# Making the row of inverse norms behind the first feature products in a hybrid RG-LRU and attention layer

## The chip, the cores and the metric

The kernel runs on one core of one Trainium2 chip. The metric is the time of one execution on the device, in microseconds (us). Engines are named as in the profile: PE is TensorE's matrix product (PEld its weight load), DVE is VectorE, ACT is ScalarE, POOL is GpSimd, SP is SyncE, whose queue issues most of the DMAs.

## The reference

One layer (DEPTH 1) over 2048 tokens of 1024 features, float32:

```python
h = rms_norm(x, norm1[l])
p = h @ w_in[l]
lru_x, lru_g, q, k, v, g, z = jnp.split(p, SPLIT_IDX, axis=-1)
lru_x = causal_depthwise_conv(lru_x, conv_w[l], conv_b[l])
lru_o = rg_lru(lru_x, ...) * jax.nn.gelu(lru_g)
...
o = gla_chunk_causal(qh, kh, vh, lah)
o = rms_norm(o, gla_norm[l]).reshape(bsz, seq, GLA_V)
gla_o = o * jax.nn.silu(g)
x = x + jnp.concatenate([lru_o, gla_o], axis=-1) @ w_out[l]
h = rms_norm(x, norm2[l])
gate, up = jnp.split(h @ w_ffn_in[l], 2, axis=-1)
x = x + (jax.nn.silu(gate) * up) @ w_ffn_out[l]
return rms_norm(x, final_norm)
```

What matters here is the first line. `rms_norm` divides each token's row by the root of its mean square and multiplies it by a gain. The division can be put behind the product with `w_in`, since it is one number per token.

## The kernel before

**Blocks and products.** The tokens are taken in four blocks (b = 0 to 3) of 512. Each product is float32 made of three passes: both operands are split into a high part (a rounding copy on ScalarE, CAST in the profile) and a low part (a subtraction on VectorE); `mm3` (L248 to L251) multiplies high by high, high by low and low by high. `split` (L256 to L260) makes the pair, so every weight and activation split has the line L259.

**Two kinds of product.** `feat` (L457) takes one unit of weights and gives a feature-major tile, 128 features by 512 tokens, in one PSUM bank: 8 chunks of 3 matmuls, 24 in all. `tokmaj` (L466) gives four token-major tiles at once, one for each 128 tokens, in four banks; it takes four units of weights and multiplies, for each unit, 2 chunks by 4 tiles by 3 matmuls, again 24. PSUM has eight banks, all from one pool (`bank`, L212).

**Weights.** `Units` (L359) feeds the units in a fixed order (`block_units`, L378): for a block the 4 units of k and z, 4 features of the recurrent part, 4 units of v, 2 features of q, then for block 0 the 4 features of the gelu gate and the 4 units of g, and for later blocks the units of the previous block's output projection among them. Each time a unit is taken, the next is loaded on SP and the second after the one taken is split, so two split units lie ahead. Weights and activations lie in two arenas, handed out in grains of 128 words a partition by `Space.alloc`; a buffer that was given back can be written once its last reader is done.

**The norm.** `Norm1` (L300) prepares the norm of one block. `chunk` (L313) splits the transposed x times the gain, which is h without the division. `scales` (L322) loads the block's four x tiles (L325), squares and sums each on ScalarE (`sumsq`, L220), makes the inverse root in eleven small VectorE operations (`rsqrt_parts`, L230), which gives `rs`, one number per token on the partitions, and then spreads it: four copies to `wide` (L335), four products of `wide` with the identity (L336), which put the numbers along the free axis in one bank, and a copy to `rb` (L339). Token-major results are multiplied by `rs`, feature-major ones by `rb`.

**Where it stands.** For block 0 `scales` is called at the end of `tokmaj_first` (L498), behind the products for k and z and ahead of the first feature product. For blocks 1 to 3 it is called in the mixer of the block before (L653), behind the products for v, the gates (`lru_gates`, L521: they run between the units of v, the last after them) and the recurrence (`lru_scan`, L537), and ahead of that block's q features (L658). Behind q come the state products (L673), and then `lru_out` in block 0 (four gelu features, L701) or `prev.half(0)` in later blocks (a `tokmaj` for half of the previous block's output projection, L715). The x tiles and the scans share the arena. In the next block k and z come first (L574), then the first recurrent feature and its convolution (L579), the transposes of z (L583), the second feature, and the small products of z (L592).

**Order.** The program is unrolled. A scheduler works out each engine's order when the kernel is built: by the order of the program, with later work ahead where it takes it to be ready sooner. `tc.issue_after(ins)` asks that what is traced inside is issued behind `ins` on that engine. On the chip each engine takes its instructions in that order and waits at the head for what is missing.

Of the kernel before, what the change touches and what calls it, by code (L numbers as in the profile page):

```python
# [15 lines left out]
P = 128  # L16
D = 1024
SEQ = 2048
T = 512
NB = SEQ // T  # L20
TT = T // P
# [157 lines left out]
def hybrid_layer_kernel(  # L179
# [20 lines left out]
    nc = tc.nc  # L200
# [3 lines left out]
    A = Arena(Space(cp.tile([P, A_GRAINS * GRAIN], F32, name="arena"), A_GRAINS), A_BORDER)  # L204
# [7 lines left out]
    def bank():  # L212
        return pp.tile([P, T], F32, tag="mm", name="mm", bufs=8)

    def small(n, name):
        return cp.tile([P, n], F32, tag=f"s{n}", name=name, bufs=10 if n < 16 else 6)

    def sumsq(dst, src, n):
        b = A.alloc(n // 2)
        nc.scalar.activation(b.ap.bitcast(BF16), src, AF.Square, accum_out=dst)  # L220
        A.free(b)

    def run(gen, n=None):
        while n is None or n > 0:
            if next(gen, run) is run:
                return
            if n is not None:
                n -= 1

    def rsqrt_parts(dst, ss, scale, n):  # L230
        v = small(n, "rv")
        nc.vector.tensor_scalar(v, ss[0], scale, EPS, op0=ALU.mult, op1=ALU.add)
        for more in ss[1:]:
            nc.vector.scalar_tensor_tensor(v, more, scale, v, op0=ALU.mult, op1=ALU.add)
        y = small(n, "ry")
        nc.vector.tensor_scalar(y.bitcast(I32), v.bitcast(I32), -0.5, 1597463007.0, op0=ALU.mult, op1=ALU.add)
        t = small(n, "rt")
        for it in range(3):
            nc.vector.scalar_tensor_tensor(t, y, -0.5, y, op0=ALU.mult, op1=ALU.mult)
            nc.vector.tensor_mul(t, t, v)  # L240
            nc.vector.scalar_tensor_tensor(dst if it == 2 else y, t, 1.5, y, op0=ALU.add, op1=ALU.mult)
            if it != 1:
                yield

    def rsqrt(*args):
        run(rsqrt_parts(*args))

    def mm3(ps, sh, sl, mh, ml, first, last, again=False):  # L248
        nc.tensor.matmul(ps, lhsT=sh, rhs=mh, start=first, stop=False, skip_group_check=again)  # L249
        nc.tensor.matmul(ps, lhsT=sh, rhs=ml, start=False, stop=False, skip_group_check=again)  # L250
        nc.tensor.matmul(ps, lhsT=sl, rhs=mh, start=False, stop=last, skip_group_check=again)  # L251

    def pair(n, low=False):
        return Pair(R, n, low)
# [16 lines left out]
    def load(src, n, low=False, queue=nc.sync):  # L271
        b = A.alloc(n, low)
        queue.dma_start(b.f(n), src)
        return b
# [14 lines left out]
    ident = cp.tile([P, P], F32, name="ident")  # L289
    rs2 = cp.tile([P, SEQ // P], F32, name="rs2")  # L290

    def cc(i):
        return col[:, i : i + 1]
# [6 lines left out]
    class Norm1:  # L300
# [18 lines left out]
            self.h.append(b)  # L319
            self.fetch()  # L320

        def scales(self):  # L322

            ss = small(TT, "ss")
            xs = [load(x_v[self.b * TT + t], D) for t in range(TT)]  # L325
            for t in range(TT):
                sumsq(ss[:, t : t + 1], xs[t].f(D), D)
            A.free(*xs)
            self.rs = cp.tile([P, TT], F32, tag="rs1", name="rs1", bufs=2)
            rsqrt(self.rs, [ss], 1.0 / D, TT)  # L330
            wide = A.alloc(T)
            ps = bank()
            for t in range(TT):
                w = wide.f(TT, P)[:, t, :]
                nc.vector.tensor_copy(w, self.rs[:, t : t + 1].to_broadcast([P, P]))  # L335
                nc.tensor.matmul(ps[:, t * P : (t + 1) * P], lhsT=w, rhs=ident, start=True, stop=True)  # L336
            A.free(wide)
            self.rb = A.alloc(T)
            nc.scalar.copy(self.rb.f(), ps)  # L339

# [116 lines left out]
    def feat(h):  # L457
        wb = feed.get()
        ps = bank()
        for c in range(KC):  # L460
            wh, wl = wb[c // 4].r(4, P)
            mm3(ps, wh[:, c % 4, :], wl[:, c % 4, :], *h[c].r(T), c == 0, c == KC - 1)
        A.free(*wb)
        return ps

    def tokmaj(h, n, between=()):  # L466
        pss = [bank() for _ in range(TT)]
        between = list(between)
        for kp in range(4):
            wb = feed.get()  # L470
            for i in range(2):
                wh, wl = wb[i].r(n)
                c = 2 * kp + i
                mh, ml = h[c].r(T)
                for t in range(TT):
                    s = slice(t * P, (t + 1) * P)
                    mm3(pss[t][:, :n], mh[:, s], ml[:, s], wh, wl, c == 0, c == KC - 1)
            A.free(*wb)
            if between:
                between.pop(0)()  # L480
        return pss

    def tokmaj_first(norm, n):

        pss = [bank() for _ in range(TT)]
        for kp in range(4):
            for _ in range(2):
                norm.chunk()
            wb = feed.get()
            for i in range(2):  # L490
                wh, wl = wb[i].r(n)
                c = 2 * kp + i
                mh, ml = norm.h[c].r(T)
                for t in range(TT):
                    s = slice(t * P, (t + 1) * P)
                    mm3(pss[t][:, :n], mh[:, s], ml[:, s], wh, wl, c == 0, c == KC - 1)
            A.free(*wb)
        norm.scales()  # L498
        return pss

    def lru_conv(b, f, ps, rb):
        raw = A.alloc(T)
        nc.vector.tensor_mul(raw.f(), ps, rb)
        ps = raw.f()
        buf = A.alloc(T)
        xc = buf.f(T)
        nc.scalar.activation(xc, ps, AF.Identity, scale=cc(C_CW + 12 + f), bias=cc(C_CB + f))
        hl = cp.tile([P, 3], F32, tag="halo", name="halo", bufs=8)
        nc.vector.tensor_copy(hl, ps[:, T - 3 : T])
        for s in (1, 2, 3):  # L510
            w = cc(C_CW + (3 - s) * 4 + f)
            nc.vector.scalar_tensor_tensor(xc[:, s:], ps[:, : T - s], w, xc[:, s:], op0=ALU.mult, op1=ALU.add)
            if b > 0:
                nc.vector.scalar_tensor_tensor(
                    xc[:, :s], halo[f][:, 3 - s : 3], w, xc[:, :s], op0=ALU.mult, op1=ALU.add
                )
        halo[f] = hl
        A.free(raw)
        return buf
# [49 lines left out]
    def mixer(b, norm, prev, side):  # L569


        kzb = A.alloc(TT * 272)
        kz = kzb.f(TT, 272)
        pss = tokmaj_first(norm, 272) if b == 0 else tokmaj(norm.h, 272, [lambda: run(side, 1)] * 4)  # L574
        h = norm.h
        for t, ps in enumerate(pss):
            nc.scalar.activation(kz[:, t, :], ps[:, :272], AF.Copy, scale=norm.rs[:, t : t + 1])
        rb = norm.rb.f()
        xcs = [lru_conv(b, 0, feat(h), rb)]  # L579
        run(side, 2)  # L580
        zps = bank()
        for t in range(TT):
            nc.tensor.transpose(zps[:16, t * P : (t + 1) * P], kz[:, t, 256:272], ident)  # L583
        nc.vector.tensor_copy(zta[:16, :], zps[:16, :])
        xcs.append(lru_conv(b, 1, feat(h), rb))
        run(side, 2)
        zfs = []
        for t2 in range(2):
            zf = bank()
            for i in range(2):  # L590
                t = 2 * t2 + i
                nc.tensor.matmul(zf[:, i * 256 : (i + 1) * 256], lhsT=zta[:, t * P : (t + 1) * P], rhs=wal,  # L592
                                 start=True, stop=True)
# [17 lines left out]
        for t2 in range(2):  # L611
            la = las[t2].f()
            sf = bank()
            for i in range(2):
                t = 2 * t2 + i
                nc.tensor.matmul(sf[:, i * 256 : (i + 1) * 256], lhsT=sfx, rhs=la[:, i * 256 : (i + 1) * 256],
                                 start=True, stop=True)
                for a in range(2):
                    nc.tensor.matmul(dview[:, a, 2 * t : 2 * t + 2],
                                     lhsT=la[:, i * 256 + a * P : i * 256 + (a + 1) * P], rhs=ind,  # L620
                                     start=True, stop=True)
# [26 lines left out]
        after = None  # L648
        if b + 1 < NB:
            after = Norm1(b + 1)  # L650
            after.fetch()
            after.fetch()
            after.scales()  # L653


        qs = []
        for a in range(2):
            ps = feat(h)  # L658
# [5 lines left out]
        for t2 in range(2):  # L664
            ups = [bank(), bank()]
            for i in range(2):
                t = 2 * t2 + i
                for hd in range(4):
                    for half in range(2):
# [5 lines left out]
                            lhsT=eks[t2].f()[s, i * 256 + hd * 64 : i * 256 + hd * 64 + 64],  # L675
                            rhs=vs[t].f()[s, hd * P : (hd + 1) * P],
                            start=True, stop=True,
# [3 lines left out]
            for i in range(2):  # L681
                t = 2 * t2 + i
# [37 lines left out]
        for t2 in range(2):  # L720
            ops = [bank(), bank()]
            for i in range(2):
                t = 2 * t2 + i
                st = sts[t].f(2, 2, P)
                for half in range(2):
                    for hd in range(4):
# [5 lines left out]
                            lhsT=qs[hd // 2].f()[s, t * P + half * 64 : t * P + half * 64 + 64],  # L732
                            rhs=st[s, half, hd // 2, :],
                            start=True, stop=True,
# [36 lines left out]
        for hd in range(4):  # L771
            ps = bank()
# [560 lines left out]
    for b in range(NB):  # L1333
        side = blocks[0].normed(b - 2) if b > 1 else iter(())
        prev, nxt = mixer(b, nxt, prev, side)
# [126 lines left out]
```

## Time and profile before

| | |
|---|---|
| median of 3 runs | 2123.89 us (2120.2 to 2124.61) |
| the profiled execution | 2116.92 us |
| its span in the profile | 2115.1 us |
| PE busy | 1996.0 us (94%) |
| DVE busy | 1357.6 us (64%) |
| ACT busy | 894.7 us (42%) |
| mean granted clock of TensorE | 0.974 of full speed |

All times in the rows are from the profiled execution, in us from the start of its span. A row of the timeline gives start, duration, engine, line, operation, output and input by name, and in brackets how long the engine had been idle before it and what ended that. Matmuls are pipelined: the distance between two starts is the price of one, not its duration. A product of float32 operands that are not split (L336, L592, L673, L878) leaves two records for each instruction.

### The profile page before, as it was taken

To read this page: it belongs to the slowest core of one execution; us is meant where nothing else is said; L and a number is where in the kernel's file an instruction comes from. 1 tells how busy PE (TensorE), PEld (TensorE's weight loads), DVE (VectorE), ACT (ScalarE), POOL (GpSimd) and SP (SyncE) were. 2 spreads that over 40 slices of the span, in tenths; PEclk is the share of its full clock that TensorE was granted. 3 is DMA by queue.
4 is the path that set the end of the run, shared out by engine and by line. 5 is a ranking of instruction groups with operands and counts; after the bars stand their busy time and mean duration, and the time that the engine had idled before them with its cause. 6 is when DMAs were issued, how large, how long until landed. Compare 5 with 4: busy or idle time off the path is not lost.

```text
span 2115.1 us, 26513 instructions
## 1 busy us (share of the span) xinstructions
PE 1996.0 (94%) x9424; PEld 1644.8 (78%) x9424; DVE 1357.6 (64%) x2411; ACT 894.7 (42%) x1513; POOL 179.4 (8%) x216
## 2 busy tenths in 40 slices
PE   7689689959998999999999999999999999999997
PEld 6568578848887887888888888888888788888876
DVE  5556555655565577656777787777776466565676
ACT  5635634662465455443344464444443211121232
POOL 0000000000000000000011101111110222222110
PEclk9889899979999999999999999999999999999999
DMA  5142145423542464466565665765765946745632
GB/s 213 60 135 97 50 141 169 165 66 118 170 150 93 136 201 156 142 194 204 182 204 187 215 194 176 236 206 195 233 214 184 393 154 209 238 149 173 228 127 80
DMA packets 215783, 361.61 MB, mean 171 GB/s; under 512 B 19921, under 2 KB 95970, under 8 KB 215650
## 3 DMA queue, kind: packets, MB, share of 16 engines
q1 hardware_dynamic: 201506, 312.71, 45.9%
q0 software_dynamic: 14144, 47.20, 5.9%
q8 instruction: 74, 1.21, 0.2%
q14 instruction: 59, 0.48, 0.1%
HBM read 252.88 MB, written 106.95 MB: 170 GB/s over the span
## 4 chain that ended last, share of the span: by engine, by line
PE 88%; DVE 4%; ACT 3%; DMA 2%; issue 2%; POOL 0%; POOLq 0%; SPq 0%; DVEq 0%; ACTq 0%
PE mm L249 29%; PE mm L250 28%; PE mm L251 28%; DMA arena_r<-w2c 1%; DMA arena<-x2d 1%; PE mm L878 1%; DVE arena L542 1%; DVE arena L1219 1%; ACT arena L220 0%; DVE arena L540 0%; ACT arena L638 0%; DVE arena L541 0%; PE mm L336 0%; DMA arena<-in_xt_dram 0%; PE mm L730 0%
## 5 line engine op out<-in xcount | busy, mean ns | idle before, releaser
L250 PE MATMUL mm<-arena_r 128*128 128x512 f32 (+1 forms) x2712 | 1047.9, 387 | 4.5 <-DVE arena_r L259 4.5
L249 PE MATMUL mm<-arena_r 128*128 128x512 f32 (+1 forms) x2667 | 1037.4, 390 | 9.1 <-DVE arena L1219 8.6
L251 PE MATMUL mm<-arena_r 128*128 128x512 f32 (+1 forms) x2715 | 1043.8, 386 | 0.0
L249 PEld LDWEIGHTS mm<-arena_r 128*128 128x128 f32 x2667 | 502.8, 189 | 128.4 <-DVE arena L1219 14.9
L251 PEld LDWEIGHTS mm<-arena_r 128*128 128x128 f32 x2715 | 511.9, 189 | 103.5
L250 PEld LDWEIGHTS mm<-arena_r 128*128 128x128 f32 x2712 | 511.6, 189 | 103.5 <-DVE arena_r L259 5.8
L259 ACT CAST arena_r<-arena 128x512 fp32r<-128x512 f32 (+1 forms) x515 | 305.1, 608 | 554.6 <-PE mm L250 247.7
L259 DVE TENSOR_TENSOR arena_r<-arena,arena_r 128x512 fp32r<-128x512 f32 (+1 forms) x509 | 336.5, 675 | 273.4 <-ACT arena_r L259 226.7
L1219 DVE TENSOR_TENSOR arena<-arena,mm 128x512 f32<-128x512 f32 x272 | 186.6, 687 | 143.4 <-PE mm L251 143.3
L1185 ACT CAST arena_r<-arena_r 128x896 fp32r<-128x896 f32 (+1 forms) x88 | 80.0, 916 | 285.6 <-PE mm L250 164.0
L1090 POOL DMA_DIRECT2D w2c<-arena x125 | 67.9, 544 | 762.3 <-ACT arena L1081 714.9
L1186 POOL TENSOR_TENSOR arena_r<-arena_r 128x896 fp32r<-128x896 f32 x40 | 84.9, 2123 | 320.9 <-PE mm L251 114.6
L259 ACT CAST arena_r<-swing 128x512 fp32r<-128x512 f32 x86 | 53.2, 621 | 94.7 <-PE mm L250 31.0
L336 PE MATMUL mm<-ident,arena 128*128 128x128 f32 x32 | 8.2, 438 | 86.8 <-issue 64.0
L336 PEld LDWEIGHTS mm<-ident,arena 128*128 128x128 f32 x32 | 7.1, 328 | 88.2 <-issue 65.0
L220 ACT ACTIVATE arena<-arena 128x512 bf16<-128x512 f32 (+1 forms) x66 | 48.2, 730 | 63.7 <-DVE arena L1219 38.8
L259 DVE TENSOR_TENSOR arena_r<-swing,arena_r 128x512 fp32r<-128x512 f32 x86 | 59.1, 688 | 24.7 <-ACT arena_r L259 17.8
L979 ACT COPY arena<-mm 128x512 f32<-128x512 f32 x98 | 57.2, 583 | 18.7 <-PE mm L251 17.8
L695 POOL COPY stc<-arena 128x256 f32<-128x256 f32 x4 | 3.7, 917 | 679.1 <-DVE arena L688 493.7
L1186 DVE TENSOR_TENSOR arena_r<-arena_r 128x896 fp32r<-128x896 f32 (+1 forms) x48 | 49.3, 1026 | 11.3 <-ACT arena_r L1185 11.2
L1002 DVE TENSOR_TENSOR arena<-mm,arena 128x512 f32<-128x512 f32 x41 | 28.3, 691 | 43.1 <-PE mm L251 43.1
L994 DVE TENSOR_TENSOR arena<-mm,arena 128x512 f32<-128x512 f32 x41 | 28.3, 690 | 35.9 <-PE mm L251 35.9
(216 smaller groups left out, 1585.7 us busy)
## 6 DMA issues: line engine op xcount, KB each, us to landing
arena_r<-w2c SPq DMA_DIRECT2D x148, 256.0 KB, 5.3
arena<-in_wgu_dram SPq DMA_DIRECT2D x144, 256.0 KB, 4.1
arena_r<-ad SPq DMA_DIRECT2D x80, 448.0 KB, 3.6
w2c<-arena POOLq DMA_DIRECT2D x125, 256.0 KB, 3.6
ad<-arena SPq DMA_DIRECT2D x120, 256.0 KB, 3.1
arena<-in_wf_dram SPq DMA_DIRECT2D x40, 512.0 KB, 3.8
arena<-in_wo_dram SPq DMA_DIRECT2D x32, 512.0 KB, 4.2
arena<-in_w_dram SPq DMA_DIRECT2D x40, 256.0 KB, 3.9
```

What stands on the lines that cost most here:

```text
L220: nc.scalar.activation(b.ap.bitcast(BF16), src, AF.Square, accum_out=dst)
L249: nc.tensor.matmul(ps, lhsT=sh, rhs=mh, start=first, stop=False, skip_group_check=again)
L250: nc.tensor.matmul(ps, lhsT=sh, rhs=ml, start=False, stop=False, skip_group_check=again)
L251: nc.tensor.matmul(ps, lhsT=sl, rhs=mh, start=False, stop=last, skip_group_check=again)
L259: b.ins = [nc.scalar.copy(hi, src).ins, nc.vector.tensor_sub(lo, src, hi.bitcast(F32)).ins]
L979: nc.scalar.copy(b.f(), ps[:, :n])
L994: nc.vector.tensor_add(u1.f(), pb[:, :n], u1.f())
L1002: nc.vector.tensor_mul(u1.f(), pa[:, :n], u1.f())
L1090: nc.gpsimd.dma_start(w2c[k][:, m, i * T : (i + 1) * T], part.f())
L1185: nc.scalar.copy(hi, v)
L1186: (nc.gpsimd if i == 1 else nc.vector).tensor_tensor(lo, v, hi.bitcast(F32), op=ALU.subtract)
L1219: nc.vector.tensor_add(c, c, ps)
```

## The change

`scales` is cut in two. `norms` keeps the loads, squares, inverse root and the four copies to `wide`, at the two places where `scales` stood. `row` does the four products, gives `wide` back and copies to `rb`; it is called in the block that uses the row, behind its first feature product, in block 0 behind its first two, and is issued behind the last matmul of the last of these products.

```diff
--- before.py
+++ after.py
@@ -245,10 +245,13 @@
     def rsqrt(*args):
         run(rsqrt_parts(*args))
 
+    latest = []
+
     def mm3(ps, sh, sl, mh, ml, first, last, again=False):
         nc.tensor.matmul(ps, lhsT=sh, rhs=mh, start=first, stop=False, skip_group_check=again)
         nc.tensor.matmul(ps, lhsT=sh, rhs=ml, start=False, stop=False, skip_group_check=again)
-        nc.tensor.matmul(ps, lhsT=sl, rhs=mh, start=False, stop=last, skip_group_check=again)
+        mm = nc.tensor.matmul(ps, lhsT=sl, rhs=mh, start=False, stop=last, skip_group_check=again)
+        latest[:] = [mm.ins]
 
     def pair(n, low=False):
         return Pair(R, n, low)
@@ -319,7 +322,7 @@
             self.h.append(b)
             self.fetch()
 
-        def scales(self):
+        def norms(self):
 
             ss = small(TT, "ss")
             xs = [load(x_v[self.b * TT + t], D) for t in range(TT)]
@@ -328,13 +331,18 @@
             A.free(*xs)
             self.rs = cp.tile([P, TT], F32, tag="rs1", name="rs1", bufs=2)
             rsqrt(self.rs, [ss], 1.0 / D, TT)
-            wide = A.alloc(T)
+            self.wide = A.alloc(T)
+            for t in range(TT):
+                nc.vector.tensor_copy(self.wide.f(TT, P)[:, t, :], self.rs[:, t : t + 1].to_broadcast([P, P]))
+
+        def row(self):
+
             ps = bank()
-            for t in range(TT):
-                w = wide.f(TT, P)[:, t, :]
-                nc.vector.tensor_copy(w, self.rs[:, t : t + 1].to_broadcast([P, P]))
-                nc.tensor.matmul(ps[:, t * P : (t + 1) * P], lhsT=w, rhs=ident, start=True, stop=True)
-            A.free(wide)
+            with tc.issue_after(latest[0]):
+                for t in range(TT):
+                    nc.tensor.matmul(ps[:, t * P : (t + 1) * P], lhsT=self.wide.f(TT, P)[:, t, :], rhs=ident,
+                                     start=True, stop=True)
+            A.free(self.wide)
             self.rb = A.alloc(T)
             nc.scalar.copy(self.rb.f(), ps)
 
@@ -495,7 +503,7 @@
                     s = slice(t * P, (t + 1) * P)
                     mm3(pss[t][:, :n], mh[:, s], ml[:, s], wh, wl, c == 0, c == KC - 1)
             A.free(*wb)
-        norm.scales()
+        norm.norms()
         return pss
 
     def lru_conv(b, f, ps, rb):
@@ -575,14 +583,16 @@
         h = norm.h
         for t, ps in enumerate(pss):
             nc.scalar.activation(kz[:, t, :], ps[:, :272], AF.Copy, scale=norm.rs[:, t : t + 1])
+        fps = [feat(h) for _ in range(2 if b == 0 else 1)]
+        norm.row()
         rb = norm.rb.f()
-        xcs = [lru_conv(b, 0, feat(h), rb)]
+        xcs = [lru_conv(b, 0, fps[0], rb)]
         run(side, 2)
         zps = bank()
         for t in range(TT):
             nc.tensor.transpose(zps[:16, t * P : (t + 1) * P], kz[:, t, 256:272], ident)
         nc.vector.tensor_copy(zta[:16, :], zps[:16, :])
-        xcs.append(lru_conv(b, 1, feat(h), rb))
+        xcs.append(lru_conv(b, 1, fps[1] if b == 0 else feat(h), rb))
         run(side, 2)
         zfs = []
         for t2 in range(2):
@@ -650,7 +660,7 @@
             after = Norm1(b + 1)
             after.fetch()
             after.fetch()
-            after.scales()
+            after.norms()
 
 
         qs = []
```

## Rows read from the trace of the kernel before

**Rows 1.** Busy times of 0 to 820 us; TensorE's timeline at its five stops.

```profile
0.00:820.00 820.00, 720.02 (x3824) 602.93 (x3825) 475.26 (x982) 420.91 (x715) 5.56 (x12) 0.94 0.41 134
...
30.04 2.05 PE L336 MATMUL mm<-ident,arena 128*128 128x128 f32 x8 [9.51 <-issue]
...
116.31 2.05 PE L336 MATMUL mm<-ident,arena 128*128 128x128 f32 x8 [27.54 <-issue]
...
270.10 2.08 PE L336 MATMUL mm<-ident,arena 128*128 128x128 f32 x8 [22.76 <-DVE arena L335]
...
476.51 2.04 PE L336 MATMUL mm<-ident,arena 128*128 128x128 f32 x8 [27.00 <-issue]
...
675.94 0.79 PE L250 MATMUL mm<-arena_r 128*128 128x512 f32 x1 [4.22 <-DVE arena_r L259]
```

**Rows 2.** Timeline of VectorE in gap 1: the last scans, the four spread copies.

```profile
102.88 2.33 DVE L542 TENSOR_TENSOR_SCAN arena<-arena 128x512 f32<-128x512 f32 x2
...
115.98 0.63 DVE L335 COPY arena<-rs 128x128 f32<-128x128 f32 x4
```

**Rows 3.** TensorE's timeline and, with its clock, one stretch: prices of matmuls.

```profile
120.66 0.40 PE L249 MATMUL mm<-arena_r,swing 128*128 128x512 f32 x1
...
121.80 0.39 PE L251 MATMUL mm<-arena_r 128*128 128x512 f32 x1
...
676.00:680.40 4.40, 4.40 (x11) 0.50 0.92 328
...
680.37 0.39 PE L249 MATMUL mm<-arena_r 128*128 128x512 f32 x1
...
397.10 1.03 PE L878 MATMUL mm<-ident,arena 128*128 128x128 f32 x8
...
130.28 1.98 PE L673 MATMUL mm<-arena 64*64 64x128 f32 x64
```

**Rows 4.** Weight splits on VectorE up to 90 us, and gap 1's timeline.

```profile
L259 DVE TENSOR_TENSOR arena_r<-arena,arena_r 128x512 fp32r<-128x512 f32 x17 | 11.5, 690 | 12.6 <-PE mm L250 6.6 <-ACT arena_r L259 3.1 <-PE mm L251 2.8
...
L259 DVE TENSOR_TENSOR arena_r<-arena,swing 128x512 fp32r<-128x512 f32 x5 | 3.4, 688 | 5.5 <-ACT swing L259 4.5 <-issue 1.0
...
L259 DVE TENSOR_TENSOR swing<-arena,arena_r 128x512 fp32r<-128x512 f32 x4 | 2.8, 688 | 1.3 <-PE mm L250 1.3
...
L259 DVE TENSOR_TENSOR swing<-arena,swing 128x512 fp32r<-128x512 f32 x2 | 1.4, 688 | 0.1
...
107.09 0.38 SPq L273 DMA_DIRECT2D arena<-in_wf_dram  x1
...
114.01 0.69 DVE L259 TENSOR_TENSOR arena_r<-arena,arena_r 128x512 fp32r<-128x512 f32 x1
...
132.19 0.50 PE L249 MATMUL mm<-arena_r,swing 128*128 128x512 f32 x1
```

**Rows 5.** Timeline around gap 2, VectorE and TensorE.

```profile
264.26 0.69 DVE L259 TENSOR_TENSOR arena_r<-arena,arena_r 128x512 fp32r<-128x512 f32 x1
...
285.94 0.50 PE L249 MATMUL mm<-arena_r 128*128 128x512 f32 x1
```

**Rows 6.** Timeline around gap 3; the page's row of such loads.

```profile
466.43 0.69 DVE L259 TENSOR_TENSOR arena_r<-arena,arena_r 128x512 fp32r<-128x512 f32 x1
...
472.35 1.98 SPq L273 DMA_DIRECT2D arena<-in_wo_dram  x2
...
arena<-in_wo_dram SPq DMA_DIRECT2D x32, 512.0 KB, 4.2
...
493.15 0.50 PE L249 MATMUL mm<-arena_r,swing 128*128 128x512 f32 x1
```

**Rows 7.** Timeline of the opening, VectorE and TensorE.

```profile
20.20 1.96 DVE L259 TENSOR_TENSOR arena_r<-arena,arena_r 128x512 fp32r<-128x512 f32 x3
...
44.92 1.99 PE L592 MATMUL mm<-arena 17*128 17x256 f32 x8
```

**Rows 8.** Timeline of VectorE in the last block.

```profile
675.86 0.69 DVE L660 SCALAR_TENSOR_TENSOR arena<-mm,arena 128x512 f32<-128x512 f32 x1
```

## The prediction, made before the change was run

> **What bounds the kernel now.** I read the idle column of the costliest groups first, then TensorE's own timeline for the places of that idle time, then the timeline of all engines in one such place, and last the weight subtractions and loads around each. TensorE is busy 94% of the span. Before 820 us it is idle for 100 us (720 of 820 are busy), and 91 of these sit in five stops. Four of them end at L336, the product that spreads the inverse norms into a row: 9.51, 27.54, 22.76 and 27.00 us, 86.8 us together. The fifth, 4.22 us, ends at a matmul that waited for a weight subtraction [rows 1]. I call the first the opening and the next three gaps 1 to 3; the fifth is the same place in the last block, where no next norm is made.
>
> What holds TensorE in gap 1 can be read in order of time: the scans (L542) run until 105.2; then come the x tiles, which are loaded into buffers that the scans give back, their squares and the inverse root; and the last spread copy (L335) ends at 116.6 [rows 2]. Not one of these operations feeds the products that stand behind L336 in TensorE's order: those read the current block's h. TensorE takes its matmuls in order, so 27 us of a chain for the *next* block stand in front of work that could run.
>
> **What the change removes.** In gaps 1 to 3 the row leaves its place; the chain itself (loads, squares, root, copies) stays where it is, with the same DMAs on the same queue. TensorE goes from the last matmul of the value stage straight to two q products, then the state updates, then the next feature products (block 0) or the output half (blocks 1, 2). At full clock a matmul starts every 0.228 us (five between 120.66 and 121.80), so a feature product of 24 costs 5.45 us; the state updates cost 1.9 us [rows 3].
>
> Gap 1: TensorE would be free at 88.8, through both q products at 99.7 and the states at 101.6. Are the next weights there? By 90 us VectorE has made 28 subtractions of 128x512 (17+5+4+2); the gate matrices, four feature units, four value units, four gates and two q units take 2+8+8+4+4 = 26. Two are left over: the first unit behind the states is ready, and it lasts until 107.1. Its successor is loaded only at 107.09 and subtracted at 114.01 to 114.70 [rows 4]. So TensorE stops for some 7.6 us and begins that second product at 114.7. Before, the first began at 132.19, hence the second at 137.6: 22.9 us earlier. From this go 2.2 us because the clock has fallen again after an idle stretch, 1.0 us for the row, which comes later, and 2 us, an estimate, because VectorE has then to catch up with evictions, states and subtractions at 0.69 us each. The clock's price is from the fifth stop: behind it the granted clock was 0.50, the lower level of 1.2 GHz, and ten matmuls from 675.94 to 680.37 took 4.43 us, against 2.28 at 2.4 GHz [rows 1, 3]. The row's price at full clock is that of eight transposing records, 1.0 us [rows 3]. Gap 1 gives 17.7 us.
>
> Gap 2: TensorE is free at 247.3, done with q and states at 260.1, and wants the first output weights, whose first subtraction ends at 264.95. The output half began at 285.94 [rows 5]: 21.0 earlier, less 2.2 and 1.0: 17.8 us.
>
> Gap 3: free at 449.5, done at 462.3, first weights at 467.12. The first unit lasts, at the low clock at first, until 474.7. The second unit is the later of two loads issued from 472.35 for 1.98 us, so at about 474; such a load lands after 4.2 us, and a cast of 0.6 and a subtraction of 0.69 make 479.8. Before, that second unit began at 493.15+5.45 = 498.6 [rows 6]. 18.8 earlier, less 2.2 and 1.0: 15.6 us.
>
> The opening: two feature products now stand ahead of the row. Their weights and those of a third are ready at 22.2 (three subtractions from 20.20), the first ones earlier, and TensorE is free at 20.5. Two products last until 31.4; the row itself could start at 30.04, so its copies are there [rows 1, 7]. So the 9.5 us are covered whole. Row 1.0, transposes of z 0.6 (an estimate from four of the eight records of [rows 3]) and a copy of about 0.7 make 33.7, where L592 started at 44.92 [rows 7]: 11.2 us. The second product's unit is taken ahead of the row, so one value-weight load on the sync queue and two casts are issued earlier; nothing else stands between on those queues.
>
> **What it adds.** In blocks 1 to 3 the first product's bank is held until row and copy (1.0+0.6 us) have passed, and the ScalarE instructions behind that copy wait with it. On TensorE the second product, 5.45 us, covers this. If that cover went, 1.6 us in each of three blocks, 5 us, would be paid. The wide buffer now lives from norm to row, and the row's buffer begins there: four grains in either case, one after the other. I cost this at nothing; between minus 5 and plus 5 us, since another place in the arena can bring a load forward or delay it by about one load (4.2 us [rows 6]).
>
> Sum: 17.7+17.8+15.6+11.2 = 62.3 us. What is late next is VectorE and the weight loads: with the gaps closed the same 475 us of VectorE work before 820 us lie in some 60 us less [rows 1]. Bounds for new waits are 0 and 10; I take 2, nearer to zero, because all that lies between the five stops has 9 us of idle TensorE, some of them before its first matmul [rows 1]. That leaves 60 us. The profiled execution took 2116.92 us (a span of 2115.1 and 1.8 around it), so it would be 2057; the median of the runs shown lies 7.0 above the profiled time, so the forecast is **2064**.
>
> **A rule against it.** The last block passes the same place, with the same eight banks, and stops for 4.22 us only [rows 1]; there the first eviction of q (L660) stands right behind the scans, at 675.86 [rows 8]. The Trainium skill, "Perfetto Trace Analysis", Optimization Strategy, says that a stop which repeats on the engine that should be saturated can mean that there is no room in SBUF or PSUM for the next tile. By that rule the gaps would come back as waits for banks, as in the first rival, and the sum would be 48 us; by the last block's row it is not so.
>
> **The rivals.** *Banks.* The q evictions could stand behind the inverse root on VectorE. Then q and the states hold six of eight banks, and the output half, which needs four, stands until both q banks are free. In gap 2 that is 270.1 (L336's start), then about five VectorE operations of 0.69: 273.5; in gap 3 476.5 and the same: 480. With half of the first twelve matmuls done, TensorE is then where it was at 287.3 and 494.5: gains of 13.8 and 14.5, less 2.2 and 1.0 each. With 11.2 for the opening and 15.7 for gap 1 (2 more of catching up), and 2 for new waits, 48 us: 2076. For it: VectorE takes its work in order. Against: [rows 8].
>
> *All hidden.* Each gap shrinks to the 4.22 us of the last block: 77.3 - 12.7 = 64.6, the opening 11.2, and three rows at 1.0 us instead of the 2.05 of the low clock 3: 79 us, 2045. Against it: the load at 107.09 and the second unit of gap 3 come late whatever TensorE does.
>
> *No change of order.* The order on each engine is worked out when the kernel is built; the row could still be put ahead of the products, and the time would stay at 2124. Against: only one matmul product is made to wait, and its place behind a named matmul is asked for.
>
> *Slower.* Place: the arena and the sync queue. The wide buffer could cut the free stretch in which weights (eight grains each) are loaded ahead, so that a load starts only when TensorE leaves the unit before. Price per unit: load 4.2, cast 0.6, subtraction 0.69 = 5.5 us of idle TensorE. From eleven units on it eats the 60 us; with 14 units the time is 2064+77 = 2141. Against it: the units are made two ahead, and the row's buffer held as many grains over the same stretch.
>
> **How the numbers follow.** Forecast 0.60, with a range of its own from 2054 to 2074 (the catching up and the new waits at their bounds); banks 0.18; all hidden 0.12; no change 0.04; slower 0.04; the last 0.02 for a small gain under 40 us. The range runs from 2045 to 2084: it takes in all hidden, the forecast and the banks with room for their own spread, and leaves out about 0.12. A measurement of this kernel can tell 0.2%, some 4 us, from no change. Faster by more: 0.92; within: 0.04; slower: 0.04.
>
> **What would show it.** In the new profile the idle time in front of L336 should be gone, and the row's eight records should take about 1.0 us behind a feature product. TensorE's idle stops should be about 8 us in gap 1 before a gelu feature's second unit, 5 in gap 2, and 5 and 5 in gap 3, each released by a weight subtraction (L259). L592 should first start near 34. If a stop is released by L660 or L688 instead, the banks decide and I was too high by some 12 us. If stops of some 5 us repeat through the value and feature stages, released by weight loads, the arena was disturbed. If the row still ends a stop, the order did not change.

## The result, and the profile after the change

The changed kernel took 2059.11 us (median of 4 runs, 2054.07 to 2064.0) against 2122.05 us (4 runs, 2117.73 to 2124.61): a ratio of 0.9705, 95% interval 0.9676 to 0.9735. The forecast was 2064. The profiled execution took 2054.07 us, with a span of 2052.3 and a mean granted clock of 0.992 (0.974 before).

The page's busy times, the kernel after:

```profile
PE 1994.5 (97%) x9424; PEld 1640.5 (80%) x9424; DVE 1354.1 (66%) x2411; ACT 896.7 (44%) x1515; POOL 182.3 (9%) x216
```

The same work on every engine, in 63 us less: all but 1.5 us of it was TensorE's idle time. Its timeline, the stops that answer to [rows 1] and two of the smaller ones between them, both in block 2:

```profile
34.93 2.25 PE L602 MATMUL mm<-arena 17*128 17x256 f32 x8 [1.72 <-DVE arena L594]
...
107.04 0.79 PE L251 MATMUL mm<-arena_r 128*128 128x512 f32 x1 [8.19 <-ACT arena_r L262]
...
237.43 0.50 PE L252 MATMUL mm<-arena_r 128*128 128x512 f32 x1 [4.22 <-DVE carry L552]
...
374.15 0.70 PE L626 MATMUL mm<-arena,sfx 128*128 128x256 f32 x2 [1.45 <-DVE arena L614]
...
386.50 0.50 PE L252 MATMUL mm<-arena_r,swing 128*128 128x512 f32 x1 [2.10 <-DVE arena_r L262]
...
426.01 0.80 PE L252 MATMUL mm<-arena_r,swing 128*128 128x512 f32 x1 [4.22 <-DVE carry L552]
...
613.02 0.51 PE L252 MATMUL mm<-arena_r 128*128 128x512 f32 x1 [4.22 <-DVE carry L552]
```

9.51, 27.54, 22.76 and 27.00 us became 1.72, 8.19, 4.22 and 4.22; the last block's 4.22 stayed. The row's products (L336 before, L343 now) no longer end a stop. The small products of z (L592 before, L602 now) are the same point of each block; their starts in blocks 1 to 3, after and then before:

```profile
175.91 1.99 PE L602 MATMUL mm<-arena 17*128 17x256 f32 x8
...
359.10 1.99 PE L602 MATMUL mm<-arena 17*128 17x256 f32 x8
...
547.24 1.99 PE L602 MATMUL mm<-arena 17*128 17x256 f32 x8
```

```profile
203.49 1.99 PE L592 MATMUL mm<-arena 17*128 17x256 f32 x8
...
404.84 1.99 PE L592 MATMUL mm<-arena 17*128 17x256 f32 x8
...
611.33 1.99 PE L592 MATMUL mm<-arena 17*128 17x256 f32 x8
```

With 34.93 against 44.92 [rows 7] in block 0, the lead is 10.0, 27.6, 45.7 and 64.1 us. So from one start to the next the lead grows by 10.0 us with the opening, 17.6 with gap 1, 18.2 with gap 2 and 18.4 with gap 3; the last block and the rest of the kernel gave 1.3 back (62.8 at the end of the span).

These steps hold everything that a block gains or loses, not the gap alone. The same matmul of both kernels, closer to a stop, shows the gap itself: the first suffix product of block 0 (these sum the log decays), the first product with the states behind gap 1, the last matmul ahead of gap 3 and the first product with the states behind it, after and then before:

```profile
49.47 0.60 PE L626 MATMUL mm<-arena,sfx 128*128 128x256 f32 x2
...
125.71 2.03 PE L740 MATMUL mm<-arena 64*64 64x128 f32 x64
...
407.94 0.39 PE L253 MATMUL mm<-arena_r 128*128 128x512 f32 x1
...
448.97 2.03 PE L740 MATMUL mm<-arena 64*64 64x128 f32 x64
```

```profile
57.88 0.60 PE L616 MATMUL mm<-arena,sfx 128*128 128x256 f32 x2
...
154.21 2.03 PE L730 MATMUL mm<-arena 64*64 64x128 f32 x64
...
449.12 0.39 PE L251 MATMUL mm<-arena_r 128*128 128x512 f32 x1
...
515.17 2.03 PE L730 MATMUL mm<-arena 64*64 64x128 f32 x64
```

The leads are 8.4, 28.5, 41.2 and 66.2 us. Of the opening's 10.0 us 1.6 are lost right behind the products of z. Gap 1 gave 20.1 and gap 3 25.0; from each some 0.9 us go for the row, which comes later in the changed kernel (the lead is 27.6 at the z products behind gap 1). Ahead of gap 3 block 2 lost 4.6 us (45.7 to 41.2), the stops at 374.15 and 386.50 among them.

### The profile page after: what moved, and what is told of

The parts are those of the page before. It is cut to its first block, busy times and chain, and to the rows that moved or that the text cites. A ratio compares the mean times of both kernels' runs of the same rounds, so it can differ in the third digit from the quotient of the medians.

```text
span 2052.3 us, 26499 instructions
## 1 busy us (share of the span) xinstructions
PE 1994.5 (97%) x9424; PEld 1640.5 (80%) x9424; DVE 1354.1 (66%) x2411; ACT 896.7 (44%) x1515; POOL 182.3 (9%) x216
## 4 chain that ended last, share of the span: by engine, by line
PE 82%; DVE 6%; DMA 5%; ACT 5%; issue 1%; POOL 0%; SPq 0%; POOLq 0%; DVEq 0%; ACTq 0%
PE mm L251 27%; PE mm L252 27%; PE mm L253 27%; DMA xq0b<-arena 1%; DMA arena<-in_wf_dram 1%; DMA arena_r<-w2c 1%; DMA arena<-in_x_dram 1%; DVE arena_r L262 1%; DMA arena<-x2d 1%; DVE arena L520 1%; ACT arena_r L262 1%; DVE arena L550 1%; PE mm L888 0%; DVE arena L1229 0%; ACT arena L648 0%
## 5 line engine op out<-in xcount | busy, mean ns | idle before, releaser
L1100 POOL DMA_DIRECT2D w2c<-arena x125 | 67.6, 541 | 763.9 <-DMA ad<-arena 374.8
L262 DVE TENSOR_TENSOR arena_r<-swing,arena_r 128x512 fp32r<-128x512 f32 x86 | 59.1, 687 | 24.7 <-ACT arena_r L262 17.8
L252 PE MATMUL mm<-arena_r,swing 128*128 128x512 f32 x112 | 45.2, 404 | 8.4 <-DVE carry L552 4.2
L251 PE MATMUL mm<-arena_r,swing 128*128 128x512 f32 x107 | 42.5, 402 | 1.0 <-ACT arena_r L262 1.0
```

Source lines behind the costliest of these rows:

```text
L262: b.ins = [nc.scalar.copy(hi, src).ins, nc.vector.tensor_sub(lo, src, hi.bitcast(F32)).ins]
L1100: nc.gpsimd.dma_start(w2c[k][:, m, i * T : (i + 1) * T], part.f())
```

## Experiments

Ratios are to the kernel before, run on the same chip beside each; its medians there were 2117.5 to 2120.2 us, so 0.001 is 2.1 us. The diffs are against the changed kernel.

**One half at a time.** The first four undo a half of the change, or move the row by one product.

e1, the opening alone:

```diff
             after.norms()
+            after.row()
...
-        fps = [feat(h) for _ in range(2 if b == 0 else 1)]
-        norm.row()
+        if b == 0:
+            fps = [feat(h) for _ in range(2)]
+            norm.row()
+        else:
+            fps = [feat(h)]
```

> Block 0 as in the change; in blocks 1 to 3 the row is made right behind the norm again, between the value and q products. Theory (each row costs what TensorE waits for it, place by place): the gaps come back with about 27, 23 and 27 us of idle TensorE ahead of the row, only the 10.0 us of the opening are kept: ratio to the kernel before 0.9953, about 2112 us. Rival (the saving hangs on the change as a whole, for instance on the clock or the layout of the buffers, and half of one edit is worth little or much more): no difference from before, or a time under 2100.

Measured: 2130.74 us, ratio 1.0053 (1.0034 to 1.0073). Neither expectation: 11 us slower than before, where 10 faster was expected. TensorE's timeline of e1 (the row is L343, the suffix products are L629):

```profile
110.23 2.05 PE L343 MATMUL mm<-ident,arena 128*128 128x128 f32 x8 [25.71 <-DVE arena L336]
...
263.86 2.05 PE L343 MATMUL mm<-ident,arena 128*128 128x128 f32 x8 [23.13 <-DVE arena L336]
...
417.62 1.22 PE L629 MATMUL mm<-arena,sfx 128*128 128x256 f32 x2 [5.42 <-DVE arena L617]
...
479.85 2.08 PE L343 MATMUL mm<-ident,arena 128*128 128x128 f32 x8 [26.55 <-DVE arena L336]
...
635.63 1.22 PE L629 MATMUL mm<-arena,sfx 128*128 128x256 f32 x2 [5.86 <-DVE arena L617]
```

The three gaps are back as the theory said, and the opening keeps 7.5 us (z products at 37.47). What it had not foreseen are the stops of 5.42 and 5.86 us ahead of the suffix products, where neither the kernel before nor the changed one stops for more than 1.5. Behind such a stop the work runs at the lower clock, as a stretch of e1 shows (length, TensorE's busy time and matmuls, granted clock, DMA share, GB/s):

```profile
417.60:426.20 8.60, 8.58 (x28) 0.50 0.09 35
```

8.6 us at half clock lose 4.3, so this stop costs 9.7 us with what follows, and from one start of the z products to the next block 2 took 11 us more than before.

e2, the gaps alone:

```diff
         norm.norms()
+        norm.row()
         return pss
...
-        norm.row()
+        if b > 0:
+            norm.row()
```

> Block 0 makes its row right behind its norm as before; blocks 1 to 3 as in the change. Theory: the opening's stop of 9.5 us ahead of the row comes back, the gaps stay closed: 10 us slower than the changed kernel, ratio to the kernel before 0.975, about 2069 us. Rival (the opening's late start would have been absorbed by later waits, for weights above all): under 2063.

Measured: 2091.43 us, ratio 0.9865 (0.9843 to 0.9888), 22 us above the theory. The opening's stop is back with 10.19 us; and again there are stops ahead of the suffix products, 5.07 and 5.99 us in blocks 2 and 3, and two of 3.74 and 1.97 for the cast of a later output unit.

e3, the row ahead of the first product in blocks 1 to 3:

```diff
+        if b > 0:
+            norm.row()
         fps = [feat(h) for _ in range(2 if b == 0 else 1)]
-        norm.row()
+        if b == 0:
+            norm.row()
```

> In blocks 1 to 3 the row is made at the head of the feature products, ahead of the first one instead of behind it; block 0 as in the change. Theory: what counts is that the row left the place between value and q products; by the next block's head its copies have been done for tens of us, so no stop ahead of the row and the time of the changed kernel, 2059 us within 3, ratio 0.970. Rival (the product ahead of the row is needed as cover in every block): about 2 us more in each of three blocks, or idle time ahead of the row, 2065 us or more.

Measured: 2078.67 us, ratio 0.9802 (0.978 to 0.9824). The number is the rival's, the mechanism is not: no row waits in blocks 1 to 3, and the time goes in stops of 4.94 and 5.59 us ahead of the suffix products and one of 4.04 for the eviction of q from its bank.

e4, one product ahead of the row in block 0:

```diff
-        fps = [feat(h) for _ in range(2 if b == 0 else 1)]
+        fps = [feat(h) for _ in range(1)]
...
-        xcs.append(lru_conv(b, 1, fps[1] if b == 0 else feat(h), rb))
+        xcs.append(lru_conv(b, 1, feat(h), rb))
```

> In block 0 one feature product instead of two stands ahead of the row. Theory: TensorE comes to the row at about 26.2 us and its copies are there at 31.6, so it stops some 5.4 us; the 1.7 us stop for the copy of z goes, since the second product now covers it: 3.7 us slower than the changed kernel, about 2063 us, ratio 0.972. Rival (one product covers the norm, as in the other blocks): no stop ahead of the row, 2057 to 2059.

Measured: 2062.99 us, ratio 0.9727 (0.9706 to 0.9748). TensorE's timeline in the opening of e4:

```profile
29.45 2.05 PE L343 MATMUL mm<-ident,arena 128*128 128x128 f32 x8 [3.08 <-issue]
...
37.80 1.99 PE L602 MATMUL mm<-arena 17*128 17x256 f32 x8
```

The row stops TensorE for 3.08 us (5.4 expected: VectorE's four weight subtractions, which stand between the steps of the inverse root in the changed kernel, from 28.29 to 31.4, come later here, so the norm itself ends earlier), the stop for z is gone, and the z products start 2.9 us later than in the changed kernel. One product does not cover the opening. The total is no clean sum: later stops differ too.

**Holding the buffers.** All four edits change when the wide buffer is given back and when the row's own buffer is handed out, and with that the places of later buffers and the order that the build works out. The next four hold this fixed: the row made early is copied back into the wide buffer, which is given back at the changed kernel's point of the program; only then is the row copied to its own buffer. They cost up to four more copies on ScalarE.

```diff
+        def row_early(self):
+
+            nc.scalar.copy(self.wide.f(), self.spread())
+
+        def row(self, early):
+
+            ps = self.wide.f() if early else self.spread()
+            old = self.wide
+            A.free(old)
             self.rb = A.alloc(T)
+            if early and self.rb.first == old.first:
+                return
...
             nc.scalar.copy(self.rb.f(), ps)
```

`spread` holds the four products. c0 calls `row_early` at both places where `scales` stood, c1 at the later blocks' alone, c2 in block 0 alone, c3 ahead of the first product of blocks 1 to 3.

> All four rows are made right behind their norms, as before the change, and kept in the wide buffer; the buffers are still given back and handed out in the changed kernel's order (the wide buffer goes back, and the row is copied to its own buffer, behind the first products). Theory (the 63 us come from the row's place on TensorE): the four stops ahead of the row are back and the time is that of the kernel before, 2122 us within 5. Rival (a good part of the 63 us is due to the new places of the buffers): clearly under 2115 us.

> The opening alone, as in e1_opening_only, but with buffers given back and handed out in the changed kernel's order. Theory (e1 lost its 20 us through the stops of 5.4 and 5.9 us ahead of the suffix products, which came with its other places of buffers): those two stops are gone, the gaps' three stops stay, about 2113 us, ratio 0.9955. Rival (the opening moved alone brings these stops in itself): the stops are there again and the time is near 2130.

> The gaps alone, as in e2_gaps_only, but with buffers given back and handed out in the changed kernel's order. Theory (the gaps are worth 54 us, the rest of e2's loss came with its places of buffers): 2069 us, ratio 0.975, no stop over 2 us ahead of the suffix products. Rival (the opening moved is needed for what follows): near 2091 as e2.

> In blocks 1 to 3 the row's products stand ahead of the first feature product, as in e3_row_ahead, but with buffers given back and handed out in the changed kernel's order. Theory (the product ahead of the row is not needed there; e3 lost through stops ahead of the suffix products, which came with its places of buffers): 2059 us within 4. Rival (the row's place ahead of the product costs the 19 us of e3 itself): near 2078.

Measured, all beside the same runs of the kernel before (2117.51 us):

| | median us | ratio, 95% | against c0 |
|---|---|---|---|
| c0, no move | 2125.52 | 1.0033 (1.0021 to 1.0046) | |
| c1, opening alone | 2114.29 | 0.9982 (0.9974 to 0.9991) | 11.2 less |
| c2, gaps alone | 2069.13 | 0.9776 (0.9763 to 0.979) | 56.4 less |
| c3, both, row ahead of the product | 2056.40 | 0.9713 (0.97 to 0.9726) | 69.1 less |

TensorE's timeline of c0, the four stops ahead of the row and one in block 2:

```profile
29.42 2.05 PE L343 MATMUL mm<-ident,arena 128*128 128x128 f32 x8 [8.38 <-issue]
...
116.92 2.04 PE L343 MATMUL mm<-ident,arena 128*128 128x128 f32 x8 [25.98 <-DVE arena L336]
...
271.86 2.08 PE L343 MATMUL mm<-ident,arena 128*128 128x128 f32 x8 [23.06 <-DVE arena L336]
...
432.47 0.50 PE L252 MATMUL mm<-arena_r,swing 128*128 128x512 f32 x1 [2.10 <-DVE arena_r L262]
...
478.66 2.04 PE L343 MATMUL mm<-ident,arena 128*128 128x128 f32 x8 [22.74 <-DVE arena L336]
```

All four stops return, and the halves add up: 11.2 and 56.4 make 67.6 of c3's 69.1. c3 carries three of c0's four extra copies and takes no more time than the changed kernel (their intervals overlap), so in blocks 1 to 3 the product ahead of the row covers nothing; there, that the row left its place between v and q is the whole effect. None of c0 to c3 stops over 1.3 us ahead of the suffix products, and the rival of c1 falls: the losses of e1 to e3 came with their buffers and orders, not with the place of the row. How, ScalarE's timeline of e1 and then of c1 shows, where the second half's absolute value of z starts (L610, and L619 there), 13.3 and 5.1 us behind the z products (398.61 and 397.82):

```profile
410.76 0.62 ACT L262 CAST arena_r<-arena 128x512 fp32r<-128x512 f32 x1 [2.29 <-DMA arena<-in_wv_dram]
...
411.87 0.58 ACT L610 ACTIVATE arena<-mm 128x512 f32<-128x512 f32 x1
```

```profile
402.87 0.59 ACT L619 ACTIVATE arena<-mm 128x512 f32<-128x512 f32 x1
```

In e1 the first half's whole chain and three weight casts stand between, the last of which, at 410.76, waits 2.29 us for its load; in c1 the second half comes ahead of most of that. So it is the order on ScalarE that differs. And c0 against before gives the price of the buffers and copies together: 4.4 to 9.7 us, a loss. How much of that is the copies was not separated.

**What stops TensorE next.** Three edits aim at the stops that are left, a fourth joins two of them.

i1, three products ahead of the row in block 0:

```diff
-        fps = [feat(h) for _ in range(2 if b == 0 else 1)]
+        fps = [feat(h) for _ in range(3 if b == 0 else 1)]
```

> In block 0 three feature products instead of two stand ahead of the row. Theory (the 1.7 us stop ahead of the small products of z is a new wait of the change, because only the row and the transposes cover the copies for z): the third product's 5.45 us now lie ahead of the row, so no stop ahead of the row, and the stop for z stays as it is, since nothing new stands between the transposes and the small products: 2058 to 2060 us. Rival (the stop goes, as the norm is over long before): its copies are then earlier than TensorE, and 1.7 to 2 us are gained.

Measured: 2059.44 us, ratio 0.9708 (0.9683 to 0.9732): no gain, as the theory had it. TensorE's timeline of i1:

```profile
39.94 1.99 PE L602 MATMUL mm<-arena 17*128 17x256 f32 x8 [0.84 <-DVE arena L594]
...
563.60 1.22 PE L626 MATMUL mm<-arena,sfx 128*128 128x256 f32 x2 [5.68 <-DVE arena L614]
```

The stop for z halved rather than stayed, and the suffix stop of e1 appeared in block 3 and took back what other stops gave.

i3, the next norm behind the first gelu features or the output half:

```diff
-            after.norms()
...
             prev.half(0)
+        if after is not None:
+            after.norms()
```

> As the change, but the next block's norm (loads of x, squares, inverse root, spread copies) is traced behind the gelu features of block 0 and behind the output half of later blocks. Theory (nothing needs the norm before the next block; gap 1's stop of 8.2 us is a weight load that stands behind x tiles on the sync queue): that stop shrinks by 5 us or more, with 2 us of low clock behind it, no row stops TensorE, about 2050 us, ratio 0.966. Rival (what counts is the room in the arena, not the order of the loads): the stop stays within 2 us of 8.2, or the later loads of x put weights late in gaps 2 and 3, 2060 us or more.

Measured: 2052.03 us, ratio 0.9676 (0.9652 to 0.9701). TensorE's timeline in gap 1:

```profile
101.82 0.61 PE L251 MATMUL mm<-arena_r 128*128 128x512 f32 x1 [2.38 <-ACT arena_r L262]
```

8.19 became 2.38, as the theory had it, and the z products of block 1 start at 170.20 instead of 175.91. In the changed kernel the load behind that stop, and the cast behind the load, are in the timelines of SP's queue and ScalarE:

```profile
101.52 0.33 SPq L276 DMA_DIRECT2D arena<-in_wf_dram  x1
```

```profile
106.37 1.66 ACT L262 CAST arena_r<-arena 128x512 fp32r<-128x512 f32 x3 [1.61 <-DMA arena<-in_wf_dram]
```

It is issued behind three loads of x (from 96.90); in i3 the two weight loads are issued from 93.36, ahead of the x tiles. The interval overlaps that of the changed kernel, so that i3 is faster is likely and not shown.

i4, the first q product ahead of the scans:

```diff
+        qps = [feat(h)]
         hs = [lru_scan(b, f, gts[f]) for f in range(4)]
...
+        qps.append(feat(h))
         for a in range(2):
-            ps = feat(h)
+            ps = qps[a]
```

> As the change, but the first q product is traced ahead of the recurrence's scans, so that the first output unit's subtraction (blocks 1 to 3) stands between the scans on VectorE instead of behind them. Theory (each of the three stops of 4.22 us is this one subtraction waiting its turn on VectorE): the three stops ahead of the first output unit go; the second unit, loaded late, stops TensorE instead in gaps 2 and 3, by 3 to 5 us, so that 4 to 12 us are gained: 2047 to 2055 us. Rival (the places of the buffers change again and bring stops of 5 us ahead of the suffix products): 2065 us or more.

Measured: 2059.7 us, ratio 0.9704 (0.9678 to 0.9729), between the two. TensorE's timeline of i4 in gap 2 and in block 3:

```profile
239.25 0.50 PE L251 MATMUL mm<-arena_r 128*128 128x512 f32 x1 [3.81 <-DVE arena L672]
...
562.92 1.22 PE L626 MATMUL mm<-arena,sfx 128*128 128x256 f32 x2 [5.84 <-DVE arena L614]
```

In gap 2 and in block 3 (3.76 us at 618.84) the subtraction no longer ends the stop; some 0.4 us less is lost to the next wait, the eviction of q from its bank (L672), which also stands behind the scans. That is the first rival of the prediction, one wait further on. In gap 3 the stop is 2.27 us.

i5, i3 with the last two scans behind the state updates:

```diff
-        hs = [lru_scan(b, f, gts[f]) for f in range(4)]
+        hs = [lru_scan(b, f, gts[f]) for f in range(2)]
...
+        hs += [lru_scan(b, f, gts[f]) for f in range(2, 4)]
         mixt = [None] * 8
```

> i3_norms_behind_half with, besides, the last two of the four scans traced behind the state updates, so that on VectorE the q evictions, the states' evictions and the first output units' subtractions stand ahead of them. Theory (the three stops of 4.2 us, and the banks that took their place in i4, are VectorE's order and nothing else): no stop over 1.5 us between the value products and the second output unit in any block, and with the low clock behind each stop 4 to 6 us gained in each of three blocks against i3: 2034 to 2042 us, ratio 0.961 to 0.964. Rival (the time goes to the next wait: the third output unit's load, which needs the buffers that the late scans give back, or other places of buffers with stops of 5 us ahead of the suffix products): 2048 us or more.

Measured: 2052.72 us, ratio 0.9685 (0.9667 to 0.9702): the rival's. TensorE's timeline of i5:

```profile
139.96 0.79 PE L251 MATMUL mm<-swing,arena_r 128*128 128x512 f32 x1 [3.59 <-ACT swing L262]
...
276.98 0.50 PE L251 MATMUL mm<-arena_r 128*128 128x512 f32 x1 [2.90 <-ACT arena_r L262]
...
279.82 0.79 PE L252 MATMUL mm<-arena_r 128*128 128x512 f32 x1 [2.34 <-DVE arena_r L262]
```

The three stops of 4.22 are gone (1.23 us is the largest left in their place), and weights that now come late, further on in the blocks, take as much. Of i3 and i5 neither is shown to be the better.

## Why the prediction was right, and where not

**The mechanism** held: the row, a product for the next block, stood at the head of TensorE's order, and c0 to c3 show its place to be worth 69 us on the changed kernel's buffers. The number, 60 us forecast and 62.9 measured, is nearer than its terms: the four places gave more than was summed, and new waits took more.

**The opening**, 10.0 of the 11.2 forecast. The row ran from 31.65 (31.4 in the forecast), but the copy for z (L594) started at 34.21, behind a subtraction and the first product with the row on VectorE, so the z products came at 34.93 and not 33.7. Behind that stop of 1.72 us the granted clock was 0.70 over 34.90 to 38.90, which the forecast had not costed, and 8.4 us were left of the lead.

**Gap 1**, 19.2 of 17.7 (20.1 less 0.9 for the row): the late load made a stop of 8.19 us where 7.6 was worked out, ended by the unit's cast and not by its subtraction. The second unit began 22.4 us earlier than in the kernel before, the opening's 8.4 left out (107.04 against 137.80), where 22.9 was forecast; the clock took 2.3 of it and the row 0.9, as costed. The 2 us for VectorE's catching up did not come. That the step of 17.6 between the z products agrees with 17.7 is luck: it holds the opening's loss of 1.6.

**Gap 2**, 18.2 of 17.8, some small losses of block 1 included: a stop of 4.22 us where some 4.8 was worked out. VectorE's timeline there:

```profile
236.69 0.68 DVE L262 TENSOR_TENSOR arena_r<-arena,arena_r 128x512 fp32r<-128x512 f32 x1
...
237.29 0.14 DVE L552 COPY carry<-arena 128x1 f32<-128x1 f32 x1
...
239.45 0.68 DVE L670 SCALAR_TENSOR_TENSOR arena<-mm,arena 128x512 f32<-128x512 f32 x1
...
240.31 0.16 DVE L232 TENSOR_SCALAR rv<-ss 128x4 f32<-128x4 f32 x1
...
240.38 0.68 DVE L670 SCALAR_TENSOR_TENSOR arena<-mm,arena 128x512 f32<-128x512 f32 x1
```

The subtraction ends at 237.37, the small carry copy behind it at 237.43, and the profile names the latter as the releaser; in c3 it names the subtraction for the same stop (238.01). The q evictions (L670) stand around the inverse root's first step and not behind the root: so the banks did not decide. The rule weighed, of the Trainium skill, "Perfetto Trace Analysis", Optimization Strategy, that a stop which repeats can mean missing room in SBUF or PSUM, is not borne out by the four stops that the change removed; i4's 3.81 us shows the room in PSUM as what waits behind them.

**Gap 3**, 24.1 where 15.6 was forecast (25.0 less 0.9 for the row; 18.4 between the z products, with block 2's losses): the step that failed is "the second unit is the later of two loads issued from 472.35". No second stop came. SP's queue in the kernel before, and in the one after:

```profile
465.37 2.10 SPq L273 DMA_DIRECT2D arena<-in_x_dram  x3
```

```profile
421.08 5.23 SPq L276 DMA_DIRECT2D arena<-in_x_dram  x5
...
427.07 1.84 SPq L276 DMA_DIRECT2D arena<-in_wo_dram  x3
```

Before, the x tiles waited for a late scan, 3.9 us behind the first carry copy (461.51); after, they start 0.7 us behind it (420.34), and the output weights are issued 5.3 us behind TensorE's halt (421.79), not 10.0 as I had it (472.35 less 462.3). c0 and c1 show that this came with the buffers and not with the row: with the row at its old place their third gap is 22.74 us, not 27.00, and in c0 the x tiles start 0.2 us behind the first carry copy (468.10 and 467.93).

**New waits and buffers** are the terms that were mis-sized. The four places together gave 69.9 us (8.4, 19.2, 18.2 and 24.1) where 62.3 was summed; with 62.8 left at the end, some 7 us went to new waits where 2 were taken (bounds 0 and 10): 4.6 us in block 2 ahead of gap 3, 1.2 between gap 3 and the next z products, 1.3 behind these. The buffers were costed "at nothing; between minus 5 and plus 5"; by c0 they and the extra copies take 8 us (4.4 to 9.7). One of the new waits is shown to be theirs: the stop of 2.10 us in block 2 (386.50) stands in c0 too (432.47), with the row at its old place, and not in the kernel before. What the others come from was not separated. So the forecast came out near because errors of opposite sign met, gap 3 and the new waits above all: that the number is so close is luck, that the gaps closed is not.

**The other cases.** *All hidden* fell with gap 1's load. *No change of order* and *Slower* fell with the timeline: the row's eight records run in 1.05 to 1.13 us (1.0 forecast) and end no stop, and no chain of weight waits formed. The terms given for *Banks* add up to 46.8 us and not 48, which changes nothing here.

## What to carry to other kernels

When an engine that takes its work in order stops, ask whether what stands at its head feeds the work behind it; here four products for the next block held back work that was ready, and moving them was worth 69 us against a control with the same buffers, 63 net in 2122. In a kernel whose buffers and order are worked out at the build, undoing half a change can also move everything else: e1 to e3 missed by 19 to 22 us until the buffers were held fixed, so a control that holds them comes first. And a stop that is removed uncovers the next wait: from 4.22 us on, four edits moved the stops and gained at most some 6 us by their ratios, which the intervals do not show.

## What the runs showed of the hardware that was not expected

The price of the low clock behind a stop was not always the 2.2 us that I took throughout. Behind the 8.19 us stop of gap 1 it was 2.3 us. Behind the 4.22 us stop in gap 2 a stretch of the changed kernel shows, in the same columns as above:

```profile
237.40:241.40 4.00, 3.97 (x10) 0.57 0.91 300
```

Some 4 us mostly at the lower level, about 1.7 us lost. Behind the 2.10 us stop in block 2 the granted clock was 1.00 over 386.50 to 390.50 in the changed kernel, and 0.65 over 432.40 to 436.40 behind the same stop of c0. Behind e1's stop of 5.42 us, where TensorE came back to the small suffix products, the granted clock was 0.50 for 8.6 us, 4.3 us lost. What makes these differences was not tested.
